# Hybrid decoder block: token sums on VectorE, g stored from GpSimd's queue, down products that share quarters taken in pairs

## The chip, the cores and the metric

One core of one Trainium2 chip runs the whole block. The metric is the device time of one execution in microseconds (us), the median of three runs. Engines: PE (TensorE matmul), DVE (VectorE), ACT (ScalarE), POOL (GpSimd), SP (SyncE, which here only issues DMAs); a q behind a name (SPq, POOLq) is that engine's DMA queue.

## The reference, cut to what matters

One block of depth 1 on 1024 tokens with 1024 features, all float32: a token mixer (pooling and sparse attention, not touched here), then the channel mixer and the last norm:

```python
def conv_ffn(xn, w_up, conv_w, conv_b, w_down):      # xn 1024x1024, D_FF = 2816
    h = xn @ w_up                                     # 1024 x 5632
    h = causal depthwise conv of width 3 over tokens (h) + conv_b
    a, b = jnp.split(h, 2, axis=-1)
    return (jax.nn.silu(a) * b) @ w_down              # 1024 x 1024

h = h + conv_ffn(rmsnorm(h, norm_ffn_g), w_up, conv_w, conv_b, w_down)
return rmsnorm(h, norm_final_g)
```

## The kernel before, in words

Everything is float32 by split operands: a value is kept as a rounded part hi (a cast on ACT, L50, L995, L1145) and the rest lo = value - hi (a subtraction on DVE or POOL, L51, L996, L1146), and a product is three matmuls, hi·hi, hi·lo, lo·hi (`mm3`, L82 to 87). The change touches the two functions of the channel mixer.

**ffn_up.** The 5632 columns of `w_up` are 44 blocks of 128, two to a chunk c (one of a, one of b). Chunk 0 (`plain`) is computed directly, as eight products. Chunks 1 to 21 (`pair`) take both blocks together with the two halves of the features and the two halves of the tokens as a 2x2 times 2x2 product in seven products in place of eight (Winograd's form). Each product is four `mm3`, so 12 matmuls of 128x128 by 128x512. For that, sums of quarters are wanted on both sides. On the weights' side each pair makes s1 to s4 (`combined`, L1070) and splits seven operands. On the tokens' side four sums T1 to T4 (for products 5, 6, 7 and 4, in the order of use) are made once, ahead of pair 1, in the loop that begins with `for k in range(4)`: T1 = x(0,1) - x(0,0), hi and lo parts alike, T2 = x(1,1) - T1, T3 = x(1,1) - x(0,1), T4 = x(1,0) - T2. T1, T2, T4 are DVE's (L1047 to L1052) and T3 POOL's; each quarter k of each sum is then split (L50, L51). The name tf stands for the float32 sums, T for the split ones. PE's products of a pair run in the order 1, 5, 2, 6, 7, 3, 4. Then `gated`: ACT applies the conv's tap of the token itself and the bias into acc (L1003), DVE adds two taps for each block (L1005, four instructions of 128x1023), ACT does silu (L1009), POOL multiplies into b (L1010), and SP stores b to the array gd in DRAM (L1011), 512 KB a chunk. The tile b has a single copy, so the next chunk's ACT step waits for that store.

**ffn_down.** g (from gd) times `w_down`, again as seven products of quarters, each over 11 blocks of the inner dimension in groups of two (five groups of two and one of one). Each group has one operand tile (`op`, three copies): quarters are loaded by SP (L1137, `raw`, twelve copies of 512 KB), POOL adds or subtracts where a product needs a sum (the `plan`, `plus`), ACT casts (L1145), DVE splits (L1146), and PE runs the group's matmuls on four banks (`steps`). In all 7 x 11 x 4 x 3 = 924 matmuls. Products 5, 6, 3 and 4 share running sums in `chs` and `cht`. The finished banks are added by DVE or POOL into h, which was loaded back from DRAM (L1202); `row_done` normalises a row with `rstd` (eleven small DVE instructions, L59 to L79) and two scalings on DVE (L1190) and stores it.

**Who sets the order.** PE's order is as written (`manual_schedule`). On all other engines a scheduler with its own cost model places the instructions, so the order of DVE, POOL, ACT and SP is not that of the code. Each engine and each queue then works strictly in that order.

## Time and profile before

| | |
|---|---|
| median of three runs | 1568.65 us (1568.16 to 1570.83) |
| the profiled execution | 1568.17 us, of which the trace's span is 1566.3 us |
| busy share of the span | PE 92%, DVE 77%, POOL 42%, ACT 41% |
| ffn_up's pairs and ffn_down | from about 849 us to the end |

The page of the profile gives busy time by engine, the span in 40 slices, the DMA queues, the chain of work that ended last, and the costliest groups of instructions. In a row of a timeline the first number is the start in us from the span's start, the second the busy us, then engine, line, operation, output<-inputs, form, count and, in brackets, the idle time before it and what ended that. Names of buffers stand without their numbers: `up` and `d` are PE's banks of the up and the down products, `w` a weight operand, `upr` a pair's loaded weights, `hr` the rows h at the end. An engine that waits shows idle time, not busy time. PE's share of 92% says little about any stage, so its waits have to be placed in time.

### The profile page before, as it was taken

The numbers are of one execution on the slowest core, as the hardware profiler recorded it, in microseconds if no ns is written. First come the engines' busy times: TensorE is split into PE (matmuls) and PEld (weight loads), VectorE is DVE, ScalarE is ACT, GpSimd is POOL, SyncE is SP. The second block draws the span as 40 slices with busy tenths as digits, with TensorE's granted clock in tenths as the row PEclk, the third lists the DMA queues.
The fourth block names the chain that finished last, engine by engine and source line by source line (L and its number), as shares of the span: only waits on it lengthen the run. The fifth ranks groups of instructions, "written<-read, shape, count | busy, mean of one in ns | idle before, by whom it ended". The sixth has DMA issues, their size and how long they took to land.

```text
span 1566.3 us, 18805 instructions
## 1 busy us (share of the span) xinstructions
PE 1433.6 (92%) x6658; PEld 1171.2 (75%) x6658; DVE 1209.4 (77%) x1875; ACT 647.0 (41%) x1111; POOL 664.4 (42%) x422
## 2 busy tenths in 40 slices
PE   6999999999899999998996499999999995898986
PEld 4887887887678788976875388888888884777765
DVE  7756999999941457876279988888888864799687
ACT  6655223213332567843033344444444433344242
POOL 4112424213522555443005754444444421778970
PEclk9999999999999999999998699999999997999998
DMA  8002423321115655166231122222222207966532
GB/s 333 8 29 91 141 76 109 123 72 41 54 74 195 186 164 162 28 214 207 86 129 40 41 81 81 81 81 81 81 81 81 81 27 292 414 220 227 202 108 108
DMA packets 77358, 193.12 MB, mean 123 GB/s; under 512 B 8784, under 2 KB 13776, under 8 KB 76752
## 3 DMA queue, kind: packets, MB, share of 16 engines
q1 hardware_dynamic: 71824, 179.34, 32.7%
q0 software_dynamic: 5440, 12.59, 2.8%
q8 instruction: 52, 0.85, 0.2%
q14 instruction: 42, 0.34, 0.1%
HBM read 148.90 MB, written 40.89 MB: 121 GB/s over the span
## 4 chain that ended last, share of the span: by engine, by line
PE 55%; DVE 30%; DMA 5%; issue 4%; POOL 3%; ACT 2%; SPq 0%; DVEq 0%; ACTq 0%; POOLq 0%
DVE tk_junk L554 11%; PE up L85 9%; PE up L87 9%; PE up L86 9%; DVE op L1146 6%; PE o L835 2%; PE pt L818 2%; PE d L86 2%; PE d L87 2%; PE d L85 2%; DVE tk_r L566 1%; DMA raw<-w_down 1%; DVE tk_cand L567 1%; PE is L439 1%; PE is L440 1%
## 5 line engine op out<-in xcount | busy, mean ns | idle before, releaser
L554 DVE TENSOR_SCALAR_CACHE_REDUCE tk_junk<-score,tk_cand 128x384 bf16<-128x384 f32 (+1 forms) x186 | 175.0, 941 | 1.8
L85 PE MATMUL up<-T,w 128*128 128x512 f32 x336 | 133.8, 398 | 30.5 <-ACT w L995 30.5
L1005 DVE SCALAR_TENSOR_TENSOR acc<-H,cw,acc 128x1023 f32<-128x1023 f32 x88 | 132.0, 1517 | 15.3 <-ACT acc L1003 14.5
L1146 DVE TENSOR_TENSOR op<-raw,op 128x1024 fp32r<-128x1024 f32 (+1 forms) x60 | 113.1, 1922 | 39.3 <-ACT op L1145 39.2
L86 PE MATMUL d<-op 128*128 128x512 f32 x308 | 125.2, 406 | 17.8 <-DVE op L1146 17.8
L85 PE MATMUL d<-op 128*128 128x512 f32 x308 | 123.7, 402 | 17.4 <-ACT op L1145 17.4
L87 PE MATMUL up<-T,w 128*128 128x512 f32 x336 | 133.6, 398 | 2.6 <-DVE w L996 2.6
L86 PE MATMUL up<-T,w 128*128 128x512 f32 x336 | 133.6, 398 | 0.0
L87 PE MATMUL d<-op 128*128 128x512 f32 x308 | 123.2, 400 | 0.0
L995 ACT CAST w<-s 128x512 fp32r<-128x512 f32 x84 | 52.0, 621 | 139.3 <-POOL s L1070 81.9
L996 DVE TENSOR_TENSOR w<-s,w 128x512 fp32r<-128x512 f32 x84 | 105.3, 1255 | 1.1
L85 PEld LDWEIGHTS up<-T,w 128*128 128x128 f32 x336 | 63.6, 189 | 46.1 <-ACT w L995 30.9
L1145 ACT CAST op<-raw 128x1024 fp32r<-128x1024 f32 (+1 forms) x60 | 56.2, 978 | 101.2 <-PE d L87 43.4
L1010 POOL TENSOR_TENSOR acc<-acc,acc 128x1024 f32<-128x1024 f32 x22 | 59.4, 2698 | 90.0 <-ACT w L995 69.6
L86 PEld LDWEIGHTS d<-op 128*128 128x128 f32 x308 | 60.0, 195 | 36.4 <-DVE op L1146 23.9
L996 POOL TENSOR_TENSOR w<-upr,w 128x512 fp32r<-128x512 f32 x23 | 36.7, 1600 | 112.4 <-DVE w L996 88.9
L85 PEld LDWEIGHTS d<-op 128*128 128x128 f32 x308 | 59.8, 194 | 31.2 <-ACT op L1145 18.3
L87 PEld LDWEIGHTS up<-T,w 128*128 128x128 f32 x336 | 63.5, 189 | 18.8 <-DVE w L996 3.4
L85 PE MATMUL up<-x2T,w 128*128 128x512 f32 x184 | 73.0, 397 | 2.3 <-ACT w L995 2.3
L86 PEld LDWEIGHTS up<-T,w 128*128 128x128 f32 x336 | 63.5, 189 | 15.2
L1070 POOL TENSOR_TENSOR s<-upr 128x512 f32<-128x512 f32 x42 | 55.9, 1331 | 42.3 <-DVE w L996 38.2
L825 DVE TENSOR_TENSOR PT<-pt,PT 128x512 fp32r<-128x512 f32 (+3 forms) x96 | 50.5, 554 | 29.8 <-ACT PT L824 29.4
(853 smaller groups left out, 4267.1 us busy)
## 6 DMA issues: line engine op xcount, KB each, us to landing
raw<-gd SPq DMA_DIRECT2D x45, 512.0 KB, 4.9
raw<-w_down SPq DMA_DIRECT2D x45, 512.0 KB, 5.5
upr<-w_up SPq DMA_DIRECT2D x44, 512.0 KB, 4.1
gd<-acc SPq DMA_DIRECT2D x22, 512.0 KB, 2.7
g<-gt SPq DMA_DIRECT2D x32, 256.0 KB, 2.0
xb<-x SPq DMA_DIRECT2D x8, 512.0 KB, 5.7
xTr<-xT SPq DMA_DIRECT2D x8, 512.0 KB, 6.4
mixd<-mixed SPq DMA_DIRECT2D x16, 256.0 KB, 2.6
```

The source lines that it names most:

```text
L85: t.matmul(ps, sh, mh, start=start, stop=False, skip_group_check=onto)
L86: t.matmul(ps, sh, ml, start=False, stop=False, skip_group_check=onto)
L87: t.matmul(ps, sl, mh, start=False, stop=stop, skip_group_check=onto)
L554: nc.vector.tensor_scalar(junk[:, :W], self.score[b], thr, None, op0=ALU.is_ge, op1=ALU.add, accum_out=cnt[:, j:j + 1])
L825: nc.vector.tensor_tensor(PT[:, j0:j1, 1, :], pt[:, 0:j1 - j0, :], PT[:, j0:j1, 0, :].bitcast(F32), op=ALU.subtract)
L995: nc.scalar.copy(t[:, 0], src)
L996: eng.tensor_tensor(t[:, 1], src, t[:, 0].bitcast(F32), op=ALU.subtract)
L1005: nc.vector.scalar_tensor_tensor(a[:, d:], H[o][:, 0:S - d], cw[:, n, 2 - d:3 - d], a[:, d:], op0=ALU.mult, op1=ALU.add)
L1010: nc.gpsimd.tensor_tensor(b, a, b, op=ALU.mult)
L1070: nc.gpsimd.tensor_tensor(t, a, b, op=op)
L1145: nc.scalar.copy(hi, val)
L1146: nc.vector.tensor_tensor(lo, val, hi.bitcast(F32), op=sub)
```

## The change

What it does, in four parts.

1. Token sums: all four on DVE, written one sum after another in the order of use (T1 and T2, then T3, then T4), with T2's float32 copy in a tile `t2f` that takes one of the two buffers of tag `raw` (the weights' of a pair). For pair 1 alone the weight sums and the last split, else POOL's, are DVE's too.
2. g is stored from POOL's queue in place of SP's.
3. ffn_down: products 1 and 5 run side by side, a group of each in turn, and 6 and 7 likewise. A quarter that both need is loaded once. All sums of quarters and all sums into h are DVE's. Four operand tiles in place of three, ten loaded quarters in place of twelve. h is loaded in four quarters of 1 MB, each written ahead of the product after which it is used.
4. The end: the last three groups in place of two are kept back and run bank by bank, the gain of the norm is multiplied ahead for two of the four quarters of h, of each row one half is scaled by ACT and one by DVE, and each half is stored by itself.

The diff, cut to its core:

```diff
@@ gated
-            nc.sync.dma_start(self.gd[c // NFH, :, :, c % NFH].rearrange("t p c -> p t c"),
-                              b.rearrange("p (t c) -> p t c", t=2))
+            nc.gpsimd.dma_start(self.gd[c // NFH, :, :, c % NFH].rearrange("t p c -> p t c"),
+                                b.rearrange("p (t c) -> p t c", t=2))
@@ ffn_up, token sums
-        for k in range(4):
-            xk = {q: [a[:, k] for a in v] for q, v in x.items()}
...
-            for n, a, b, eng in ((1, xk[0, 1], xk[0, 0], nc.vector), (3, xk[1, 1], xk[0, 1], nc.gpsimd)):
-                eng.tensor_tensor(f[n], a[0], b[0], op=sub)
-                eng.tensor_tensor(f[n], f[n], a[1], op=ALU.add)
-                eng.tensor_tensor(f[n], f[n], b[1], op=sub)
...
+        t2 = fw.tile([P, 4, HB], F32, tag="raw", name="t2f")
+        def difference(n, k, a, b):
+            f = pool.tile([P, HB], F32, tag=f"s{n}", name=f"tf{n}_{k}")
+            tt_(f, a[0], b[0], op=sub)
+            tt_(f, f, a[1], op=ALU.add)
+            tt_(f, f, b[1], op=sub)
+            return f
...
+        for k in range(4):
+            f = difference(1, k, xk((0, 1), k), xk((0, 0), k))
+            keep(1, k, f)
+            less(t2[:, k], xk((1, 1), k), f)
+            keep(2, k, t2[:, k])
+        for k in range(4):
+            keep(3, k, difference(3, k, xk((1, 1), k), xk((0, 1), k)))
+        for k in range(4):
+            f = pool.tile([P, HB], F32, tag="s4", name=f"tf4_{k}")
+            less(f, xk((1, 0), k), t2[:, k])
+            keep(4, k, f)
@@ pair
-                nc.gpsimd.tensor_tensor(t, a, b, op=op)
+                (nc.gpsimd if c > 1 else nc.vector).tensor_tensor(t, a, b, op=op)
...
-            operand_of(4, A[1, 1], nc.gpsimd)
+            operand_of(4, A[1, 1], nc.gpsimd if c > 1 else nc.vector)
@@ ffn_down
-        add, sub, plus = ALU.add, ALU.subtract, nc.gpsimd.tensor_tensor
+        add, sub, tt = ALU.add, ALU.subtract, nc.vector.tensor_tensor
...
+        def prepare_1_5(j, n):
+            A, B = quarters(j, n)
+            s, t = cs[:, j:j + n], ct[:, j:j + n]
+            p1, p5 = operand(1, j, n), operand(5, j, n)
+            put(p1, 0, A(0, 0))
+            b = B(0, 0)
+            put(p1, 1, b)
+            put(p5, 0, combined(s, A(1, 0), A(1, 1), add))
+            put(p5, 1, combined(t, B(0, 1), b, sub))
+            return p1, p5
...
+        def prepare_6_7(j, n):
...
+            a, b = A(0, 0), B(1, 1)
+            put(p6, 0, combined(s, s, a, sub))
+            put(p6, 1, combined(t, b, t, sub))
+            put(p7, 0, combined(a, a, A(1, 0), sub))
+            put(p7, 1, combined(b, b, B(0, 1), sub))
+            return p6, p7
...
-        def run(p, ps, first):
-            tail = 2 if p == 4 else 0
+        def run(prepare, pss, fresh, tail=0):
...
+                for t, ps in zip(ts, pss):
                     for tb in range(4):
-                        steps(ps, t, n, tb, first, k == 0, k == len(groups) - 1)
+                        steps(ps, t, n, tb, fresh, k == 0, k == len(groups) - 1)
...
+        def load_h(th, dh):
+            cols = slice(dh * HB, (dh + 1) * HB)
+            nc.sync.dma_start(h[:, 4 * th:4 * th + 4, cols], ...)
...
+            for dh in (1 - scaled, scaled):
+                q, cols = quarter(th, dh, tb), slice(dh * HB, (dh + 1) * HB)
+                if dh == scaled:
+                    nc.scalar.activation(q, q, AF.Copy, scale=y)
+                else:
+                    nc.vector.scalar_tensor_tensor(q, q, y, gfin[:, cols], op0=ALU.mult, op1=ALU.mult)
+                nc.sync.dma_start(io["out"][b * P:(b + 1) * P, cols], q)
...
-            run(1, x, True)
+            x, y = banks("x", 1), banks("y", 5)
+            run(prepare_1_5, (x, y), True)
...
-            run(4, x, False)
+            run(prepare_4, (x,), False, 3)
```

How it moves instructions, at three places.

DVE, where the token sums begin. `x2T1a` and `x2T1b` are the last token block of x, whose halves the sums wait for; before:

```order
L139 TENSOR_TENSOR x2T1a_7341<-hpt7_0_7598,x2T1a_7341 128x4x128
L1047 TENSOR_TENSOR tf1_0_7710<-x2T1a_7341,x2T00_6849 128x512
L139 TENSOR_TENSOR x2T1b_7342<-hpt7_4_7605,x2T1b_7342 128x4x128
L1048 TENSOR_TENSOR tf1_0_7710<-tf1_0_7710,x2T1a_7341 128x512
L1049 TENSOR_TENSOR tf1_0_7710<-tf1_0_7710,x2T10_6850 128x512
L1051 TENSOR_TENSOR tf2_0_7711<-x2T1b_7342,tf1_0_7710 128x512
L51 TENSOR_TENSOR T1_7706<-tf1_0_7710,T1_7706 128x512
```

and now:

```order
L139 TENSOR_TENSOR x2T1a_7341<-hpt7_0_7598,x2T1a_7341 128x4x128
L1048 TENSOR_TENSOR tf1_0_7711<-x2T1a_7341,x2T00_6849 128x512
L139 TENSOR_TENSOR x2T1b_7342<-hpt7_4_7605,x2T1b_7342 128x4x128
L1048 TENSOR_TENSOR tf3_0_7751<-x2T1b_7342,x2T1a_7341 128x512
L1049 TENSOR_TENSOR tf1_0_7711<-tf1_0_7711,x2T1a_7341 128x512
L1049 TENSOR_TENSOR tf3_0_7751<-tf3_0_7751,x2T1b_7342 128x512
L1050 TENSOR_TENSOR tf1_0_7711<-tf1_0_7711,x2T10_6850 128x512
L1050 TENSOR_TENSOR tf3_0_7751<-tf3_0_7751,x2T1a_7341 128x512
L1054 TENSOR_TENSOR t2f_7710<-x2T1b_7342,tf1_0_7711 128x512
L51 TENSOR_TENSOR T1_7706<-tf1_0_7711,T1_7706 128x512
L1055 TENSOR_TENSOR t2f_7710<-t2f_7710,x2T1b_7342 128x512
L51 TENSOR_TENSOR T3_7708<-tf3_0_7751,T3_7708 128x512
```

T3's sums, POOL's before, stand between T1's and T2's, in every quarter k. The end of the sums, now (before, `w1_5`, the operand of pair 1's product 5, stood two rows behind the last T2 split, and its sum s1 was POOL's):

```order
L51 TENSOR_TENSOR T1_7706<-tf1_3_7741,T1_7706 128x512
L51 TENSOR_TENSOR T3_7708<-tf3_3_7769,T3_7708 128x512
L1055 TENSOR_TENSOR t2f_7710<-t2f_7710,x2T1b_7342 128x512
L1086 TENSOR_TENSOR s1_1_7805<-upr1_7797 128x512
L1086 TENSOR_TENSOR s3_1_7818<-upr1_7797 128x512
L1054 TENSOR_TENSOR tf4_3_7790<-x2T00_6849,t2f_7710 128x512
L1086 TENSOR_TENSOR s2_1_7810<-s1_1_7805,upr1_7797 128x512
L51 TENSOR_TENSOR T2_7707<-t2f_7710,T2_7707 128x512
L996 TENSOR_TENSOR w1_5_7807<-s1_1_7805,w1_5_7807 128x512
```

The row of `w1_5` is the 64th, counted from the first sum, and T4's sums for k = 0 to 2 are done before it.

SP, where the down products begin. `gd` is g in DRAM, `raw` a loaded quarter (side and quarter in its name), `hr` h; before:

```order
L1011 DMA gd_7548<-acc43_10796 128x2x512
L1137 DMA raw1_000_10833<-gd_7548 128x1024
L1137 DMA raw1_010_10837<-w_down 128x1024
L1137 DMA raw1_200_10866<-gd_7548 128x1024
L1137 DMA raw1_210_10870<-w_down 128x1024
```

and now:

```order
L988 DMA upr21_10657<-w_up 128x1024 x2
L1226 DMA hr_10816<-hd_97 128x4x512
L1263 DMA gfin_10817<-norm_final_g 128x1024
L1226 DMA hr_10816<-hd_97 128x4x512 x3
L1138 DMA rawg00_0_10834<-gd_7548 128x1024
L1138 DMA raww00_0_10838<-w_down 128x1024
L1138 DMA rawg10_0_10842<-gd_7548 128x1024
L1138 DMA rawg11_0_10844<-gd_7548 128x1024
L1138 DMA raww01_0_10849<-w_down 128x1024
```

All of h and the gain stand ahead of the first quarter, directly behind the last weights, and the store of the last g is on POOL's queue. Quarter `g11` is the first that contains the last chunk of g.

DVE, at the end. `d7_3` is the last bank, f3 to f7 are rows 3 to 7 in `rstd`; before:

```order
L1234 TENSOR_TENSOR hr_10819<-d7_2_11687,hr_10819 128x512
L67 SCALAR_TENSOR_TENSOR f4t_12400<-f4y_12399,f4v_12398 128x1
L78 TENSOR_SCALAR f4t_12400<-f4t_12400 128x1
L59 TENSOR_SCALAR f5v_12418<-ssf5_11916 128x1
L79 TENSOR_TENSOR f4y_12399<-f4y_12399,f4t_12400 128x1
L1190 SCALAR_TENSOR_TENSOR hr_10819<-hr_10819,f4y_12399,gfin_10820 128x512 x2
L62 TENSOR_SCALAR f5t_12420<-f5v_12418 128x1
L1234 TENSOR_TENSOR hr_10819<-d7_3_11688,hr_10819 128x512
```

and now:

```order
L1298 TENSOR_TENSOR hr_10816<-d7_2_11451,hr_10816 128x512
L67 SCALAR_TENSOR_TENSOR f3t_12155<-f3y_12154,f3v_12153 128x1
L74 TENSOR_SCALAR f3u_12156<-f3t_12155 128x1
...
L79 TENSOR_TENSOR f3y_12154<-f3y_12154,f3t_12155 128x1
L1251 SCALAR_TENSOR_TENSOR hr_10816<-hr_10816,f3y_12154,gfin_10817 128x512
L62 TENSOR_SCALAR f4t_12368<-f4v_12366 128x1
L1298 TENSOR_TENSOR hr_10816<-d7_3_11452,hr_10816 128x512
L63 TENSOR_SCALAR f4y_12367<-f4t_12368 128x1
```

Before the last bank's sum stood row 4's scaling; now row 3's stands there and row 4's comes behind.

## Rows read from the trace of the kernel before

**Rows 1.** What PE waited for, 840 to 1567 us: total us, times, longest.
```profile
PE up L85 <- ACT w L995: 30.5, 1, 30.5
PE d L86 <- DVE op L1146: 17.8, 11, 3.4
PE d L85 <- ACT op L1145: 17.4, 2, 15.9
```

**Rows 2.** PE's timeline at the first up pair and the first down product.
```profile
879.37 0.79 PE L85 MATMUL up<-T,w 128*128 128x512 f32 x1 [30.46 <-ACT w L995]
...
883.24 0.80 PE L87 MATMUL up<-T,w 128*128 128x512 f32 x1 [2.65 <-DVE w L996]
...
1309.41 0.80 PE L85 MATMUL d<-op 128*128 128x512 f32 x1 [15.93 <-ACT op L1145]
```

**Rows 3.** DVE's timeline in the token sums.
```profile
831.36 0.68 DVE L1047 TENSOR_TENSOR tf<-x2T1a,x2T 128x512 f32<-128x512 f32 x1
...
837.67 1.77 DVE L1052 TENSOR_TENSOR tf<-tf,x2T1b 128x512 f32<-128x512 f32 x1
...
868.25 2.83 DVE L51 TENSOR_TENSOR T<-tf,T 128x512 fp32r<-128x512 f32 x1
```

**Rows 4.** Timelines of POOL and ACT, in the token sums and around the last chunk.
```profile
867.74 2.78 POOL L1010 TENSOR_TENSOR acc<-acc,acc 128x1024 f32<-128x1024 f32 x1
...
876.96 3.40 POOL L1070 TENSOR_TENSOR s<-upr 128x512 f32<-128x512 f32 x2
...
1298.83 2.34 POOL L1010 TENSOR_TENSOR acc<-acc,acc 128x1024 f32<-128x1024 f32 x1 [16.59 <-DVE acc L1005]
...
1294.73 1.24 ACT L1003 ACTIVATE acc<-H,cb,cw 128x1024 f32<-128x1024 f32 x1 [1.96 <-DVE H L1098]
...
1309.56 1.05 ACT L1145 CAST op<-raw 128x1024 fp32r<-128x1024 f32 x1 [0.20 <-DMA raw<-gd]
```

**Rows 5.** SP's timeline after the last chunk; the second number is the issue.
```profile
1301.20 0.36 SPq L1011 DMA_DIRECT2D gd<-acc  x1
...
1304.38 0.35 SPq L1137 DMA_DIRECT2D raw<-w_down  x1
```

**Rows 6.** DVE's timeline in the down products.
```profile
1309.39 6.23 DVE L1146 TENSOR_TENSOR op<-raw,op 128x1024 fp32r<-128x1024 f32 x5 [1.13 <-ACT op L1145]
...
1348.06 3.38 DVE L1146 TENSOR_TENSOR op<-cht,op 128x1024 fp32r<-128x1024 f32 x1
```

**Rows 7.** Windows: us, busy (x) of PE, PEld, DVE, ACT, POOL, PEclk, DMA, GB/s.
```profile
1309.00:1316.00 7.00, 6.13 (x14) 4.46 (x15) 6.12 (x5) 4.54 (x5) 0.00 (x0) 0.50 1.02 420
1340.00:1380.00 40.00, 35.61 (x155) 28.47 (x154) 31.02 (x14) 17.86 (x23) 31.34 (x12) 1.00 0.91 358
...
1309.40:1552.00 242.60, 222.96 (x924) 178.38 (x924) 198.47 (x163) 90.46 (x120) 167.41 (x64) 0.96 0.64 235
```

**Rows 8.** PE's timeline in the up products, 32 matmuls from the first to the last.
```profile
886.50 0.40 PE L86 MATMUL up<-T,w 128*128 128x512 f32 x1
...
893.97 0.40 PE L85 MATMUL up<-T,w 128*128 128x512 f32 x1
```

**Rows 9.** DMA issues: output<-input, queue, count, KB each, median us to landing.
```profile
upr<-w_up SPq DMA_DIRECT2D x44, 512.0 KB, 4.1
gd<-acc SPq DMA_DIRECT2D x22, 512.0 KB, 2.7
...
qA<-qd POOLq DMA_DIRECT2D x16, 256.0 KB, 3.7
...
mx<-mixd POOLq DMA_DIRECT2D x4, 1024.0 KB, 10.3
```

**Rows 10.** DVE's timeline at the end.
```profile
1552.33 0.68 DVE L1234 TENSOR_TENSOR hr<-d,hr 128x512 f32<-128x512 f32 x1
...
1554.57 1.41 DVE L1190 SCALAR_TENSOR_TENSOR hr<-hr,f5y,gfin 128x512 f32<-128x512 f32 x2
...
1557.73 1.41 DVE L1190 SCALAR_TENSOR_TENSOR hr<-hr,f6y,gfin 128x512 f32<-128x512 f32 x2
```

More of the change, by code (lines that the diff above doesn't have):

```diff
@@ L1203, in ffn_down @@
-            for tb in range(4):
-                nc.scalar.copy(r5[:, tb], y[tb])
-            run(2, x, False)
+                nc.scalar.copy(u2[:, tb], x[tb])
+            load_h(0, 0)
+            for tb in range(4):
+                nc.scalar.copy(u4[:, tb], y[tb])
+            run(prepare_2, (x,), False)
+            nc.sync.dma_start(gfin, io["norm_final_g"].partition_broadcast(P))
+            load_h(1, 1)
             for tb in range(4):
                 q = quarter(0, 0, tb)
-                nc.vector.tensor_tensor(q, x[tb], q, op=add)
+                tt(q, x[tb], q, op=add)
@@ L1209, in ffn_down @@
                 half_done(0, 0, tb)
-            y = banks("y", 6)
-            run(6, y, True)
+                gain(0, 0, tb)
+            y, x = banks("y", 6), banks("x", 7)
+            run(prepare_6_7, (y, x), True)
+            load_h(0, 1)
             for tb in range(4):
-                nc.vector.tensor_tensor(u2[:, tb], y[tb], r1[:, tb], op=add)
-                plus(r5[:, tb], r5[:, tb], u2[:, tb], op=add)
-                for th, dh, u in ((1, 1, r5), (0, 1, r5), (1, 0, u2)):
-                    q = quarter(th, dh, tb)
-                    plus(q, q, u[:, tb], op=add)
@@ L1224, in ffn_down @@
+                tt(q, q, u4[:, tb], op=add)
             y = banks("y", 3)
-            run(3, y, True)
+            run(prepare_3, (y,), True)
+            load_h(1, 0)
+            for tb in range(4):
+                q = quarter(1, 0, tb)
+                tt(q, q, u2[:, tb], op=add)
             for tb in range(4):
                 q = quarter(0, 1, tb)
-                nc.vector.tensor_tensor(q, y[tb], q, op=add)
+                tt(q, y[tb], q, op=add)
                 half_done(0, 1, tb)
-                row_done(0, tb)
```

119 lines of the change are left out of this document (62 added, 57 removed).

## Prediction

> **What bounds the kernel now.** I read the waits of the matrix engine (PE) first, over the last 727 us. Nearly all its idle time there is in three places [rows 1, 2]: one wait of 30.5 us and one of 2.6 us where the second half of the network (the up products) begins, 17.4 us on ACT's casts of which 15.9 stand in one piece where the down products begin, and eleven short ones, 17.8 us in all, on DVE's splits inside the down products.
>
> The first place: PE resumes at 883.24 [rows 2]. The operand it waits for is made from a weight sum that POOL begins at 876.96, because POOL first finishes its share of the token sums [rows 4]. DVE meanwhile is busy without a pause, but at two speeds: a 128x512 sum takes 0.68 us while POOL is idle and 1.77 us beside a POOL sum; beside POOL's 2.78 us product one split took 2.83 us [rows 3, 4].
>
> The second place: the last up product ends at about 1293.5, its g leaves POOL at 1301.2 (1298.83 + 2.34), and only then does SP, which stores g, come to the loads behind the store; the second load waits for the store to land and goes at 1304.38, and PE starts at 1309.41 [rows 2, 4, 5].
>
> The third place: a 128x1024 split takes 1.22 us when POOL is idle (6.12 us for five, with the DMA engines moving 420 GB/s) and 3.38 us beside a POOL sum [rows 6, 7]. So both engines crawl in step, and PE waits for each second operand. After the 15.9 us gap PE's granted clock is 0.50, so 1.2 in place of 2.4 GHz: 14 matmuls in 6.13 us, 0.44 each [rows 7], where 32 in the up products take 7.47 us, 0.233 each [rows 8]. In all the 924 matmuls of the down products stand in 242.6 us [rows 7]; at 0.233 they would take 215.6, so 27.0 us are lost there.
>
> **Token sums (first place).** POOL's 16 instructions go to DVE; it issues 56 in place of 40, and pair 1's four weight sums and one split as well. The order shown above is not the order of use: T3's sums stand beside T1's and T4's between them, and the first operand of product 5 is the 64th row counted from the first sum. Those are 60 of 128x512 and four convolution steps of 128x1023. At the undisturbed rate (0.61 and 1.22 us, a fifth of the five splits) that is 36.6 + 4.9 = 41.5 us. The first sum stands at 831.36 [rows 3]; it moves about 1 us ahead, since pair 1's first split and four matmuls no longer stand before it. One POOL piece is left in this stretch, the product of plain chunk 0, which costs DVE 2.83 - 0.61 = 2.2 us. So 830.4 + 41.5 + 2.2 = 874.1, against 883.24: 9.1 us saved. ACT must keep up: chunk 0's accumulator needs PE's last blocks. PE's long wait begins at 879.37 - 30.46 = 848.9 [rows 2], after pair 1's first 12 matmuls (2.8 us), so those blocks are there near 846, while DVE comes to that row after 20 sums, near 842.6; at worst DVE waits 5 us there (gain 4). With no POOL product at all the gain would be 11. The float32 copy of T2 also takes one of the two weight buffers, so pair 2's weights are loaded only after T4, and land 4.1 us later [rows 9], near 880; PE comes to pair 2 about 17 us after 874, and the sixth product of pair 1 waits at most a microsecond longer behind DVE's first pair-2 splits. **Term: -9, between -11 and -4.**
>
> **g stored from POOL's queue.** In the up products PE is never short of anything, so 21 of the 22 stores only change places. The buffer of b has one copy: ACT fills it at 1294.73, the store goes at 1301.20 and lands 2.7 us later, 9.2 us in all [rows 4, 5, 9], of a pair's 84 matmuls of 0.233 us = 19.6 us [rows 8]. There are 10 us of slack, and an issue on POOL adds about half a microsecond.
>
> **Start of the down products (second place).** By the order, SP now issues four 1 MB loads of h and the gain first, as soon as T2's and T3's buffers are free, at two and three products of 2.8 us before the up products end (near 1285 and 1288 on the old clock), then three quarters that wait for the last up product alone, and then one that waits for the last store. 4.7 MB at 358 GB/s [rows 7] is 13 us, so h is in near 1299, the first two quarters 2.9 us later, and with some 1 us to land and a cast of 1.05 [rows 4] PE begins near 1304: 5 us ahead of 1309.41. Its first 24 matmuls last 14 x 0.44 + 10 x 0.233 = 8.5 us, to 1312.5. Product 5's first operand hangs on the last store. No row has a store of 512 KB from POOL; the nearest are 2.7 us for the same tile from SP and 3.7 us for a 256 KB load from POOL [rows 9]; I take 3.7. Then 1301.2 + 0.5 + 3.7 + 4.1 (load) + 2.4 (two sums) + 1.05 (cast) + 1 (the split before) = 1314, so 1.5 us of wait. **Term: -4;** h at 420 GB/s and a quick store give -8, h at 300 GB/s and a store like the 10.3 us of the 1 MB loads from POOL give +3. The Trainium skill, page "DMA: Bandwidth & Descriptors", section "Anatomy of one DMA — SWDGE (gpsimd) path", fits such a transfer as 2.0 us plus bytes over 436 GB/s, an estimate of 3.2 us here; by it the term would be -4.5. No run so far shows it.
>
> **Down products (third place).** Products 1 and 5 now share the load of B(0,0), 6 and 7 those of A(0,0) and B(1,1): 15 loads of a group in place of 18. All 48 combinations go from POOL to DVE, and POOL has no row left after the last store. DVE's load: 84 splits and 48 sums, 110 of 128x1024 and 22 of half that, 121 x 1.22 = 148 us; 44 sums of 128x512 for h, u2 and u4, 27 us; four of the eight row scales, about 10 us. That is 185 us beside PE's 215.6 us. By stage: products 1 and 5, 6 rows of 1.22 in 11.2 us of PE; 2, 2.4 in 5.6; 6 and 7, 8 rows, 9.8 in 11.2; 3 and 4, 3.7 in 5.6 and the h sums besides. The tightest is products 6 and 7, where some of their sums already stand within product 2 in DVE's order, and four operand buffers hold two pairs. ACT casts 14 rows a group, 14.7 us in 39. So I take the waits of this stage as gone, and the slow clock behind them: of the 27.0 us lost only the slow start stays, 14 x (0.44 - 0.233) = 2.9 us, which leaves 24. I keep 2 us for waits that I don't see. **Term: -22,** between -24 (none) and -12 (half stay).
>
> **The end.** The last group is kept back over three groups in place of two, and half of each row is scaled by ACT. Before, the last sum from PSUM starts at 1552.33 and the rows follow at 3.16 us each [rows 10], to the span's end at 1566.3, 14 us. In the order, rows 4 to 7 still stand behind the last sum from PSUM, row 4 whole where before it was half done; each is shorter by one 0.7 us scale. One row more and 4 x 0.7 less: **0, within 1.5.**
>
> **Sum.** -9 - 4 - 22 + 0 = -35. The profiled execution took 1568.17 us with a span of 1566.3, so 1531.3 + 1.9 = 1533 us. The median of the three runs is 0.5 us above that execution, which changes nothing here.
>
> **Rivals.**
> *DVE is late in spite of its average* (chance 0.09). It works in order, and its order puts sums far ahead of splits that PE needs now; in product 3 some 20 h sums stand between two splits. For it: the average load is 86%. Against it: by stage it stays under PE's time. If half of the third place's gain is lost: 1545 us.
>
> *The transfers bind* (0.06). Products 1 and 5 ask for 5 x 0.52 MB in 11.2 us, 234 GB/s, after 4.7 MB of h. If the chip gave 250 GB/s, h would land 5.7 us later, the first ten quarters 6 us later, and what is lost would not be made up before product 2: some 18 us, 1551. Against it: 358 and 420 GB/s in the rows [rows 7].
>
> *Stores from POOL starve* (0.04), the one that ends slower. The place is the single buffer of b. If a store lands more than 2.7 + 10 = 12.7 us after its product, ACT waits, then DVE, then PE, in each of 21 pairs. The nearest row with a bad value is 10.3 us, for 1 MB loads four at a time [rows 9]. Each microsecond beyond 12.7 costs 21; from 14.4 on the whole gain of 35 is gone, and at 16 the time is 1533 + 69 = 1602. The Trainium skill, page "SBUF — State Buffer", section "Who interferes with whom", says that a DMA which seems stalled by a DVE operation was issued by GpSimd and starved of descriptor time. The same section adds, as inferred, that a tensor_tensor does not do this, and DVE has mostly those here. The rows agree so far in that loads from POOL beside a busy DVE land in 3.7 us.
>
> *Nothing moves* (0.01): each gain is eaten by a wait right behind it, 1568.
>
> **How the numbers follow.** My forecast has 0.80. Its own terms reach from -47 to -15, and all at one end is unlikely, so I take 1524 to 1542 for it. With the late DVE the range is 1524 to 1549, which leaves out the other rivals and a little of the forecast. A measurement here tells 0.2%, about 3 us: faster 0.80 + 0.09 + 0.06 = 0.95, same 0.01, slower 0.04.
>
> **What would show it.** PE's wait before product 5 of pair 1 about 24 us, and DVE's 128x512 sums near 0.68 us throughout. A first down matmul about 11 us after the last up matmul, then one wait of 1 to 3 us. DVE's splits of 128x1024 near 1.2 us with no POOL rows beside them, and no wait of PE above 1 us until the end. The end about as long as before. I am wrong if PE waits for DVE in products 6, 7 or 3, if the h loads hold the first operand beyond 14 us, or if accumulators wait for stores.

## The result, and the profile after

The changed kernel takes 1533.32 us (median of 4 runs, 1530.82 to 1533.77), the kernel before beside it 1568.41 us (4 runs, 1567.64 to 1570.83): 0.977 of it, with an interval of 0.9753 to 0.9787. 1533 was forecast. The profiled execution took 1532.94 us with a span of 1530.8, against 1566.3 before: 35.5 us less. The whole came out as forecast. Of its terms one, the down products, came out beyond its range, and the token sums gave back part of what they had won.

What PE waited for in the same stretch as in [rows 1], 830 us to the end, after the change (total us, times, longest):

```profile
PE up L85 <- ACT w L995: 20.3, 1, 20.3
PE d L85 <- ACT op L50: 11.6, 2, 10.7
...
PE d L86 <- DVE op L51: 1.3, 2, 0.8
...
```

The wait of 30.5 us is 20.3, the 15.9 before the down products 10.7, and the eleven waits on splits, 17.8 us, are two of 0.8 and 0.5. One wait has grown: before product 3 of pair 1, the sixth of that pair's seven, PE lost 1.2 us, now 2.5.

That wait before, and PE's timeline after, where [rows 2] answer to it, with that wait and the first down products:

```profile
896.77 0.47 PE L85 MATMUL up<-x2T1b,w 128*128 128x512 f32 x1 [1.24 <-DVE u L1092]
```

```profile
872.99 0.79 PE L85 MATMUL up<-T,w 128*128 128x512 f32 x1 [20.34 <-ACT w L995]
875.35 0.79 PE L87 MATMUL up<-T,w 128*128 128x512 f32 x1 [1.14 <-DVE w L996]
891.47 0.77 PE L85 MATMUL up<-x2T1b,w 128*128 128x512 f32 x1 [2.53 <-DVE u L1108]
...
1300.40 0.80 PE L85 MATMUL d<-op 128*128 128x512 f32 x1 [10.69 <-ACT op L50]
...
1309.25 0.50 PE L85 MATMUL d<-op 128*128 128x512 f32 x1 [0.86 <-ACT op L50]
1310.57 0.50 PE L86 MATMUL d<-op 128*128 128x512 f32 x1 [0.81 <-DVE op L51]
```

DVE's timeline after in the token sums (answers to [rows 3]):

```profile
860.15 0.69 DVE L1054 TENSOR_TENSOR t2f<-x2T1b,tf 128x512 f32<-128x512 f32 x1
...
878.34 2.75 DVE L1086 TENSOR_TENSOR s<-upr,s 128x512 f32<-128x512 f32 x1
881.83 4.18 DVE L996 TENSOR_TENSOR w<-s,w 128x512 fp32r<-128x512 f32 x1 [0.74 <-ACT w L995]
```

POOL's there (answers to [rows 4]):

```profile
858.00 22.53 POOL L1010 TENSOR_TENSOR acc<-acc,acc 128x1024 f32<-128x1024 f32 x1 [30.32 <-DVE acc L1005]
...
881.65 2.56 POOL L1086 TENSOR_TENSOR s<-upr 128x512 f32<-128x512 f32 x2
```

DVE keeps one speed, 0.60 us from start to start, from 834 to 878. But POOL's one product there, 2.78 us before, takes 22.5 us, and pair 2's weight sums stand behind it. It ends beside DVE's next row, at 878.34, which takes 2.75 us in place of 0.69, and beside POOL's first weight sums for pair 2 DVE's split at 881.83 takes 4.18.

SP's timeline from the last up products (answers to [rows 5]), and the DMA issues of g (answers to [rows 9]; KB each, median us to landing):

```profile
1284.56 1.54 SPq L1226 DMA_DIRECT2D hr<-hd  x3
...
1291.37 10.82 SPq L1138 DMA_DIRECT2D rawg<-gd  x2
```

```profile
gd<-acc POOLq DMA_DIRECT2D x22, 512.0 KB, 3.2
```

DVE in the down products (answers to [rows 6]), and windows with the columns of [rows 7]: the first 40 us of the down products and all of them.

```profile
1341.77 1.22 DVE L51 TENSOR_TENSOR op<-cht,op 128x1024 fp32r<-128x1024 f32 x1
```

```profile
1300.00:1340.00 40.00, 37.47 (x148) 29.79 (x149) 32.87 (x30) 16.90 (x18) 0.00 (x0) 0.90 0.96 370
1300.40:1516.50 216.10, 213.73 (x924) 175.47 (x924) 174.03 (x221) 92.72 (x124) 0.00 (x0) 0.98 0.59 202
```

No row of 3.38 us is left: all splits and sums of 128x1024 take 1.22. What a matmul of the down products takes where PE does not wait is read from the starts. PE's timelines, 32 matmuls from the first row of each view to the second, before and then after:

```profile
1320.65 0.39 PE L85 MATMUL d<-op 128*128 128x512 f32 x1
...
1327.91 0.39 PE L87 MATMUL d<-op 128*128 128x512 f32 x1
```

```profile
1450.14 0.39 PE L85 MATMUL d<-op 128*128 128x512 f32 x1
...
1457.40 0.39 PE L87 MATMUL d<-op 128*128 128x512 f32 x1
```

In both kernels that is 7.26 us, 0.227 each; in the up products it is 7.47 us, 0.233 each [rows 8], and so it is after.

The end after, DVE's last sum from PSUM (answers to [rows 10]):

```profile
1516.31 0.69 DVE L1298 TENSOR_TENSOR hr<-d,hr 128x512 f32<-128x512 f32 x1 [0.51 <-PE d L87]
```

**By stage.** A span is cut at four places: t0, the start of DVE's last split of a token block (line 139, 830.75 us before); the end of the last up matmul; the end of the last down matmul; the end of the span. What lies before t0 is the same code in all kernels here, and yet t0 falls between 829.7 and 839.6, so small totals are read by stage. Each ratio is to the runs of the kernel before that were made beside that kernel.

| kernel | t0 | t0 to the last up matmul | to the last down matmul | to the end | median us (runs) | ratio, interval |
|---|---|---|---|---|---|---|
| before | 830.75 | 462.74 | 258.21 | 14.60 | 1568.41 (4) | |
| after | 833.60 | 456.11 | 226.56 | 14.53 | 1533.32 (4) | 0.977, 0.9753 to 0.9787 |
| tsums | 830.03 | 461.09 | 254.12 | 14.86 | 1566.74 (12) | 0.9984, 0.9966 to 1.0002 |
| sp_store | 829.73 | 459.73 | 228.26 | 14.68 | 1536.49 (3) | 0.9792, 0.9769 to 0.9815 |
| c0_dve | 839.62 | 453.19 | 224.48 | 14.61 | 1529.79 (4) | 0.9746, 0.9721 to 0.9771 |
| t_order | 830.49 | 468.70 | 224.68 | 14.53 | 1541.64 (6) | 0.9825, 0.9796 to 0.9854 |
| t_order_c0 | 834.52 | 467.18 | 224.45 | 14.55 | 1542.13 (4) | 0.9829, 0.9807 to 0.985 |
| down_pool | 831.57 | 456.12 | 253.96 | 13.05 | 1561.22 (4) | 0.9946, 0.9925 to 0.9967 |
| woven | 831.48 | 455.89 | 224.48 | 14.55 | 1530.26 (4) | 0.9761, 0.9728 to 0.9793 |
| gd_split_h_late | 830.93 | 456.12 | 226.21 | 14.64 | 1531.08 (4) | 0.9763, 0.9738 to 0.9788 |
| b_low | 837.65 | 454.60 | 221.39 | 14.56 | 1525.9 (4) | 0.9717, 0.9684 to 0.9749 |
| tail_rows | 834.34 | 456.17 | 230.88 | 9.41 | 1531.73 (4) | 0.9755, 0.9736 to 0.9773 |
| all_three | 832.52 | 451.81 | 221.78 | 9.39 | 1517.29 (5) | 0.9666, 0.9651 to 0.968 |

Where the code of a stage is the same, the up stage agrees within 0.06 us (after, down_pool, gd_split_h_late, tail_rows), the down stage within 2.1 (after, c0_dve, t_order, t_order_c0, woven). One kernel stands apart: b_low's edit adds no instruction to the up stage, and that stage is 1.5 us shorter. PE's timeline of b_low at product 3 of pair 1:

```profile
895.53 0.47 PE L85 MATMUL up<-x2T1b,w 128*128 128x512 f32 x1 [3.27 <-DVE u L1111]
```

Product 3 starts 57.9 us after t0 there, as in the changed kernel. But the row lasts 0.47 us in place of 0.77: the granted clock stayed at 1.00 over the wait, where in the changed kernel it stood at 0.50 for some 3 us behind it. So 1.5 us of an up stage can come or go with the clock alone.

### The profile page after: what moved, and what is told of

It reads as the page before. It is cut to its first block, busy times and chain, and to the rows that moved or that the text cites. A ratio compares the mean times of both kernels' runs of the same rounds, so it can differ in the third digit from the quotient of the medians.

```text
span 1530.8 us, 18757 instructions
## 1 busy us (share of the span) xinstructions
PE 1431.6 (94%) x6658; PEld 1173.2 (77%) x6658; DVE 1177.1 (77%) x1960; ACT 652.7 (43%) x1119; POOL 491.8 (32%) x359
## 4 chain that ended last, share of the span: by engine, by line
PE 64%; DVE 26%; DMA 3%; issue 3%; ACT 3%; POOL 1%; SPq 0%; DVEq 0%; ACTq 0%; POOLq 0%
DVE tk_junk L554 11%; PE up L85 9%; PE up L86 9%; PE up L87 9%; PE d L86 4%; PE d L87 4%; PE d L85 4%; PE o L835 2%; PE pt L818 2%; DVE tk_r L566 2%; DVE tk_cand L567 1%; PE is L439 1%; PE is L440 1%; PE wvp L86 1%; PE wvp L85 1%
## 5 line engine op out<-in xcount | busy, mean ns | idle before, releaser
L85 PE MATMUL up<-T,w 128*128 128x512 f32 x336 | 134.0, 399 | 20.3 <-ACT w L995 20.3
L85 PE MATMUL d<-op 128*128 128x512 f32 x308 | 121.4, 394 | 11.6 <-ACT op L50 11.6
L86 PE MATMUL d<-op 128*128 128x512 f32 x308 | 121.3, 394 | 1.3 <-DVE op L51 1.3
L87 PE MATMUL d<-op 128*128 128x512 f32 x308 | 120.8, 392 | 0.0
L1010 POOL TENSOR_TENSOR acc<-acc,acc 128x1024 f32<-128x1024 f32 x22 | 79.1, 3593 | 120.5 <-ACT w L995 70.8
L85 PE MATMUL up<-x2T,w 128*128 128x512 f32 x184 | 74.4, 405 | 2.3 <-ACT w L995 2.3
L86 PEld LDWEIGHTS up<-T,w 128*128 128x128 f32 x336 | 63.7, 190 | 15.2
L87 PE MATMUL up<-x2T,w 128*128 128x512 f32 x184 | 74.1, 403 | 0.0
L86 PE MATMUL up<-x2T,w 128*128 128x512 f32 x184 | 74.1, 402 | 0.0
L1003 ACT ACTIVATE acc<-H,cb,cw 128x1024 f32<-128x1024 f32 x44 | 54.8, 1246 | 35.6 <-DVE H L1114 24.4
```

What stands on the lines that cost most here:

```text
L85: t.matmul(ps, sh, mh, start=start, stop=False, skip_group_check=onto)
L86: t.matmul(ps, sh, ml, start=False, stop=False, skip_group_check=onto)
L87: t.matmul(ps, sl, mh, start=False, stop=stop, skip_group_check=onto)
L1003: nc.scalar.activation(a, H[o], AF.Identity, bias=cb[:, n:n + 1], scale=cw[:, n, 2:3])
L1010: nc.gpsimd.tensor_tensor(b, a, b, op=ALU.mult)
```

## The experiments

**tsums: the token sums alone.** The kernel before with the first part of the change; the stores stay on SP, the down products as they were.

```diff
+        t2 = fw.tile([P, 4, HB], F32, tag="raw", name="t2f")
...
+        for k in range(4):
+            f = difference(1, k, xk((0, 1), k), xk((0, 0), k))
+            keep(1, k, f)
+            less(t2[:, k], xk((1, 1), k), f)
+            keep(2, k, t2[:, k])
...
-                nc.gpsimd.tensor_tensor(t, a, b, op=op)
+                (nc.gpsimd if c > 1 else nc.vector).tensor_tensor(t, a, b, op=op)
```

> The kernel before with the first part of the change alone: token sums all on DVE, t2f in a weight buffer, pair 1's weight sums and last split on DVE. Theory A (the prediction): the part is worth 9 us, 1568.4 - 9 = 1559.4. Theory B, from the trace of the changed kernel: from the first token sum to the last up product it has 455.5 us where before had 462.1, so 6.6 us, 1561.8, because POOL's product of chunk 0 lasts 22.5 us beside a DVE that never pauses, POOL's weight sums of pair 2 come late, and product 3 of pair 1 waits 2.5 us. Below 1560.5 speaks for A, above for B. By both DVE's 128x512 sums take about 0.69 us throughout; B also expects POOL's product of chunk 0 to last over 15 us here.

Both theories miss. The first operand comes 9.2 us earlier, as in the whole change (t0 + 39.37 against + 48.62), and POOL's product is as long as theory B has it, but the stage is only 1.65 us shorter, and the median does not tell it from before. SP's and POOL's timelines of tsums show what takes it back:

```profile
876.97 0.38 SPq L1011 DMA_DIRECT2D gd<-acc  x1
877.40 25.75 SPq L988 DMA_DIRECT2D upr<-w_up  x6
```

```profile
854.42 22.52 POOL L1010 TENSOR_TENSOR acc<-acc,acc 128x1024 f32<-128x1024 f32 x1 [29.57 <-DVE acc L1005]
884.61 2.49 POOL L1086 TENSOR_TENSOR s<-upr 128x512 f32<-128x512 f32 x2 [7.67 <-DMA upr<-w_up]
```

Chunk 0's product takes 22.52 us on POOL, SP waits with its store at the head of the queue, and pair 2's weight loads stand behind that store. POOL then waits 7.67 us for them and PE 6.60 before product 3 of pair 1.

**sp_store: the whole change with the store back on SP.**

```diff
-            nc.gpsimd.dma_start(self.gd[c // NFH, :, :, c % NFH].rearrange("t p c -> p t c"),
+            nc.sync.dma_start(self.gd[c // NFH, :, :, c % NFH].rearrange("t p c -> p t c"),
```

> The changed kernel with one edit undone: g is stored from SP's queue again. In SP's order the store of chunk 0 then stands ahead of the loads of pair 2's weights, and the last store ahead of the first quarter of the down products. Theory A (the prediction): 21 of the 22 stores only change places, so from the last token block's first split on DVE to the end of the last up product the stage stays at 456 us, as in the changed kernel; only the start of the down products changes. Theory E: pair 2's weights are loaded only when POOL has finished the product of chunk 0, which DVE starves; the stage becomes as long as in the run with the token sums alone, 461 us, and POOL waits some 8 us for weights. By both the gap between up and down products grows from 10.7 to about 15 us, and product 5 follows with a shorter wait. Total by A 1534 to 1537, by E 1539 to 1542.

SP's timeline in sp_store shows the same queue as in tsums:

```profile
876.68 0.38 SPq L1011 DMA_DIRECT2D gd<-acc  x1
877.12 2.95 SPq L988 DMA_DIRECT2D upr<-w_up  x4
```

In the changed kernel those loads go 41.1 us after t0 (874.72), here 47.4 us after it, and POOL waits 7.6 us for them. The up stage, 459.73 us, is 3.6 us longer, nearer to theory E; the total lies in A's range. The gap between up and down products is 15.3 us, as both had it, and the down stage is 1.7 to 3.8 us longer than the five readings of the same code. So POOL's queue for the store is worth some 5 to 7 us in these traces; the medians differ by 3.2, with intervals that overlap.

**c0_dve: chunk 0's product on DVE.**

```diff
-            nc.gpsimd.tensor_tensor(b, a, b, op=ALU.mult)
+            (nc.vector if c == 0 else nc.gpsimd).tensor_tensor(b, a, b, op=ALU.mult)
```

> The changed kernel with one instruction moved: the product of chunk 0 (silu(a) * b) by DVE in place of POOL. Theory A: DVE's list before product 5 gets 1.2 us longer, no wait goes away: 1533.3 to 1534.5. Theory B: POOL is free when pair 2's weights land, its weight sums and DVE's splits come earlier, the 2.5 us wait at product 3 of pair 1 goes with about 1.6 us of slow clock behind it, less 1.2 us: about 3 us faster, 1530.4.

The first operand comes 1.1 us later (t0 + 40.51), by the product that now stands in DVE's row. But the wait before product 3 falls from 2.53 to 0.56 us, and the stage from 456.11 to 453.19, 9.55 us below before. PE's and DVE's timelines of c0_dve there:

```profile
896.07 0.47 PE L85 MATMUL up<-x2T1b,w 128*128 128x512 f32 x1 [0.56 <-DVE u L1108]
```

```profile
885.48 0.69 DVE L1086 TENSOR_TENSOR s<-upr,s 128x512 f32<-128x512 f32 x1
886.91 1.51 DVE L996 TENSOR_TENSOR w<-s,w 128x512 fp32r<-128x512 f32 x1 [0.74 <-ACT w L995]
```

The two rows of DVE that took 2.75 and 4.18 us take 0.69 and 1.51, and product 3 starts 56.5 us after t0 in place of 57.9. This shows that the starved product made PE wait longer there, worth 1.4 us. The other 1.5 us are the clock behind that wait (the row lasts 0.47 us in place of 0.77): b_low got them with the product starved and a longer wait, so c0_dve does not show that they belong to the product.

**t_order: DVE's token sums strictly in the order of the code; t_order_c0: the same with chunk 0's product on DVE.**

```diff
+        def tt_(*args, **kw):
+            then(nc.vector.tensor_tensor(*args, **kw))
...
-            self.split(f, T[n][:, 0, k], T[n][:, 1, k])
+            nc.scalar.copy(T[n][:, 0, k], f)
+            tt_(T[n][:, 1, k], f, T[n][:, 0, k].bitcast(F32), op=sub)
```

> The changed kernel with the token sums chained in the order that the code writes, T1 and T2, then T3, then T4; nothing else is tied, other DVE work may stand between. The operand of product 5 becomes the 39th row counted from the first sum, in place of the 64th. Theory C: PE's wait for product 5 sets this stage; that product starts about 12 us earlier, PE then waits for T3 and T4 in smaller pieces, the last of T4 ends where it ended, product 3 starts some 8 us earlier: 1525. Theory D: the length of the whole list sets it, the last T4 split and the weights of pair 2 that wait for the buffer of t2f end where they did, so pair 2 starts no earlier: 1531 to 1533.

> Both of the two edits before: token sums chained in written order, and the product of chunk 0 by DVE. Theories B and C together: 8 + 3 us, 1522. If B is wrong and C right, 1525 to 1526. If C is wrong (theory D) and B right, 1530. POOL's weight sums of pair 2 should begin when its weights land, and product 3 of pair 1 should not wait for a DVE sum for more than 1 us.

Both miss: the first operand comes earlier by 5.9 and 6.9 us (t0 + 33.49, + 32.48), and the stage is 12.6 and 11.1 us longer. DVE's, PE's and POOL's timelines of t_order:

```profile
858.55 0.69 DVE L1054 TENSOR_TENSOR tf<-tf,x2T1a 128x512 f32<-128x512 f32 x1
859.27 0.69 DVE L1054 TENSOR_TENSOR tf<-tf,x2T 128x512 f32<-128x512 f32 x1
860.65 0.69 DVE L1054 TENSOR_TENSOR T<-tf,T 128x512 fp32r<-128x512 f32 x1 [0.69 <-ACT T L1069]
...
894.26 0.69 DVE L1098 TENSOR_TENSOR s<-upr,s 128x512 f32<-128x512 f32 x1
```

```profile
895.71 0.79 PE L85 MATMUL up<-x2T1b,w 128*128 128x512 f32 x1 [7.01 <-ACT w L995]
```

```profile
854.74 2.63 POOL L1010 TENSOR_TENSOR acc<-acc,acc 128x1024 f32<-128x1024 f32 x1 [29.41 <-DVE acc L1005]
```

A sum that needs the one before it starts 0.72 us after it, not 0.60, and each split waits some 0.7 us for ACT's cast of the sum just made. The list gets longer: the last split of T4 ends 63.7 us after t0, in the changed kernel 44.7. Two of pair 1's own weight sums stand behind T3's and T4's sums (882.24 and 894.26), and PE waits 7.26 and 7.01 us for the operands made from them; t_order_c0 has the same two waits. T2's copy also holds its weight buffer longer, and pair 2's weights come late: POOL gets them at 896.92, in the changed kernel it began at 881.65. In the changed kernel the mixed order covers both pauses: its rows start every 0.60 us. In the pauses POOL's product takes 2.63 us: it is not the product that is slow.

**down_pool: the 48 quarter sums of the down products back on POOL.** Pairing, shared loads and row scales stay as changed.

```diff
-            tt(dst, a, b, op=op)
+            nc.gpsimd.tensor_tensor(dst, a, b, op=op)
```

> The changed kernel with the 48 sums of quarters of the down products back on POOL, the shared loads, the pairing and the sums into h as changed. Theory A (the prediction): a split beside a POOL sum takes 3.4 us in place of 1.2, 48 of them, so PE waits again in most groups of products 5, 6, 7, 3 and 4; from the first to the last down matmul 230 to 243 us (before 242, changed 216). Theory F: sharing and pairing are what removed the waits, and POOL's sums run in the pauses of DVE: 216 to 222 us.

The down stage is 253.96 us, against 258.21 before and 226.56 changed. DVE's and POOL's timelines of down_pool:

```profile
1341.85 2.32 DVE L51 TENSOR_TENSOR op<-cht,op 128x1024 fp32r<-128x1024 f32 x1
1344.09 1.21 DVE L51 TENSOR_TENSOR op<-rawg,op 128x1024 fp32r<-128x1024 f32 x1
```

```profile
1340.81 2.28 POOL L1149 TENSOR_TENSOR cht<-raww,raww 128x512 f32<-128x512 f32 x1
```

Beside POOL's sum a split takes 2.32 us (others up to 3.4), as soon as POOL is idle 1.21. The down matmuls take 243.7 us from first to last, just above theory A's range and far from F's. The 4.3 us that are left against before are the earlier start (a gap of 10.28 for 15.92 us); the matmuls themselves take 1.4 us more than before. So the gain of the down products themselves is that POOL has no row there; products that share loads bring nothing without it. What they bring together with it was not tried apart.

**gd_split_h_late: g in one scratch tensor for each two chunks, and the loads of SP in the order of the code, h behind the first quarters.**

```diff
-        self.gd = dram("gd", [2, 2, P, NFH, HB])
+        self.gd = {(f, j): dram(f"gd{f}{j}", [2, P, min(2, NFH - j), HB]) for f in range(2) for j in range(0, NFH, 2)}
...
+        def fetch(dst, src):
+            ins = nc.sync.dma_start(dst, src)
+            if loads:
+                self.tc.add_manual_dep(ins.ins, loads[-1].ins.name,
...
```

> The changed kernel with two edits at the start of the down products: g in DRAM as one array for each half and group in place of a single one, so that a quarter waits only for the stores that it holds; and SP's loads of ffn_down tied in the order of the code, so that the 4 MB of h and the gain come after the quarters of products 1 and 5. Theory H: h ahead of the quarters holds PE's start by about 4 us, and the last store holds product 5: the gap between up and down falls from 10.7 to about 7 us, product 5 starts without a wait, the first 24 matmuls are followed at once; span about 5 to 6 us less in these two stages (gap + down 226.6 us in the changed kernel, now 221). Theory I: the transfers bind here anyway (404 GB/s in the gap): the h loads only move into products 1 and 5 and make PE wait there, gap + down 225 to 227.

The gap before the first down matmul falls from 10.69 to 6.8 us, but the matmuls then take 219.40 us from first to last, in place of 215.87: 226.21 in all, no gain, as theory I has it. SP's timeline of this kernel:

```profile
1288.70 10.80 SPq L1137 DMA_DIRECT2D rawg<-gd  x2
```

SP still stands 10.8 us at the third quarter of g, though nothing that the last store writes is read by it any more. So it did not wait for the data. By the layout its buffer overlaps the last chunk's b, which the last store still reads, so it may wait for space; the next run tries that.

**b_low: the same, with b's buffer placed where no early quarter overlaps it.**

```diff
+        for o in (1, 0):
+            pool.tile([P, S], F32, tag=f"acc{o}", name=f"place{o}")
```

> As gd_split_h_late, with the tile of b placed first in its pool, by allocating its tag ahead of the others; no instruction is added. Theory J: in the changed kernel and in gd_split_h_late the load of quarter g11 of the first group waits for the last store not for its data but for its space: its buffer overlaps the tile of b, which the store reads (addresses 113408 to 117504 against 110048 to 114144), and all later loads stand behind it on SP. With b lower, the first six quarters wait for nothing later than DVE's last read of the H tiles, some 5 us after the last up product; product 5 then follows the first group of product 1 without a wait above 0.5 us, gap + down 226.2 us in gd_split_h_late becomes about 222. Theory I: the transfers bind in products 1 and 5, PE waits for quarters somewhere there, gap + down stays 225 to 227.

SP's timeline of b_low:

```profile
1293.90 3.85 SPq L1139 DMA_DIRECT2D rawg<-gd  x2
```

PE now has two waits, 7.5 us before the first operand and 1.3 at the second, the one before product 5 is gone, and the stage takes 221.39 us, 4.8 less than gd_split_h_late, as theory J has it. It was space. (That its up stage is shorter too is not the edit's doing, see By stage.)

**tail_rows: rows 0 to 3 of the last norm taken as one batch, ahead of DVE's wait for the last product.**

```diff
+                if tb == 0:
+                    ss["y"] = self.rstd(pool, ss["all"], "f03", n=4, halves=True)
+                y = ss["y"][:, tb:tb + 1]
```

> The changed kernel with the last norm's rows 0 to 3 taken together: their eleven small instructions once for four rows in place of four times, all ahead of the first sum of product 4 on DVE. Theory K: in the changed kernel DVE stood 2.8 us at the first of product 4's sums with rows 1 to 3 queued behind it, so rows 4 to 7 came after the last sum, 14.5 us from the last matmul to the end. Now each of rows 4 to 6 is done while PE works on the next bank, one row is left behind the last sum: 8 to 9 us from the last matmul to the end, the whole 6 us less than the changed kernel. Theory L: the end is set by the stores and the wait for them, 12 us or more.

The end is 9.41 us, 5.1 less, near the 8 to 9 of theory K. But the down stage grew to 230.88 us, 4 to 6 more than its like. SP's timeline of tail_rows, and its window to set beside the changed kernel's first 40 us:

```profile
1306.55 0.48 SPq L1141 DMA_DIRECT2D rawg<-gd  x1
...
1308.86 6.56 SPq L1229 DMA_DIRECT2D hr<-hd  x3
```

```profile
1300.00:1340.00 40.00, 34.85 (x124) 27.17 (x125) 22.04 (x20) 12.17 (x12) 0.02 (x1) 0.85 0.97 378
```

With this edit the order of SP's loads, which the build sets, came out otherwise: h stands among the quarters that products 1 and 5 wait for. From 1300 to 1340 PE made 124 matmuls, in the changed kernel 148. That the new place of h is the cause was not tried by itself.

**woven: two blocks of sums side by side in a fixed order, chunk 0's product on DVE.** Each block's rows stand between the other's, so that no sum follows the one it needs.

```diff
+        def spare(n, k):
+            tag = {1: ("s3", "s4"), 2: ("u2", "u4"), 3: ("s3", "s4"), 4: ("r1", "s4")}[n][k % 2]
+            return pool.tile([P, HB], F32, tag=tag, name=f"tf{n}_{k}")
...
+        for thread in (first, third, fourth):
+            weave(thread, (0, 1))
+            weave(thread, (2, 3))
```

> As c0_dve, with the token sums tied in an order of use that weaves two quarters k: T1 and T2 of k 0 and 1, then of k 2 and 3, then T3, then T4, in two threads, so that a split never stands right behind its own sum; pair 2's splits stand behind pair 1's sums from PSUM. The tiles of the float32 sums take other tags so that two of a kind can be live. Theory G (why the written order was slower): there each split waited about 0.7 us for ACT's cast of the sum just before it, and each sum for the one before; woven, the list is as short as in the changed kernel (T4's last split about 45 us after the first), product 5 starts about 26 us after the first split of the last token block in place of 40, and the stage to the end of the last up product is 448 to 450 us (c0_dve 453.2, changed 456.1). Theory D: the length of DVE's whole list sets the end, pair 1's last products still wait for it: 452 to 454 us, with more and shorter waits of PE.

The stage takes 455.89 us, no better than the changed kernel and outside both theories. PE's longest wait says why:

```profile
PE up L85 <- ACT r L1148: 19.5, 1, 19.5
```

That was a slip in the edit: half of T4's sums lie in the buffer r1, which ACT needs for the copies out of PSUM, so PE's next chunk waited for the last token sums. The run says nothing on the order itself.

**all_three: woven without that slip, with the edits of b_low and of tail_rows.** T4's sums lie in a buffer of chunk 0's accumulator.

```diff
+        four = pool.tile([P, S], F32, tag="acc0", name="tf4")
+        weave(fourth, (0, 1))
+        weave(fourth, (2, 3))
```

> The changed kernel with all repairs: the product of chunk 0 by DVE, the token sums woven by two quarters in the order of use (T4's float32 sums in a tile of the accumulators, so that no tile that pair 1 needs early is held), pair 2's splits behind T4; the start of the down products as in b_low; the end as in tail_rows. From the first split of the last token block to the end of the last up product: theory G (the list is as short as the changed one's, products 5, 2, 6, 7, 3 run while it ends) 448 to 450 us, theory D (DVE's whole list sets the end) 452 to 454, changed 456.1. With J and K, total about 17 us below the changed kernel, 1516; with D, I and L about 3 below, 1530.

What PE waited for in all_three, 830 to 1300 us:

```profile
PE up L88 <- ACT w L1000: 6.9, 1, 6.9
...
PE up L89 <- DVE T L1054: 4.1, 1, 4.1
PE up L88 <- ACT r L1157: 3.7, 1, 3.7
...
PE up L88 <- DVE u L1163: 1.2, 1, 1.2
PE up L90 <- DVE w L1001: 0.5, 1, 0.5
```

Three waits of 23.9 us in the up products have become five of 16.4 us, 4.3 us of the stage against the changed kernel and only 1.4 against c0_dve, no more than the clock alone made in b_low. The stage, 451.81 us, lies below D's 452 to 454 and above G's 448 to 450. DVE's list is not shorter for the weaving: the last split of T4 ends 50.9 us after t0, in c0_dve 45.8. So that the order itself brings anything is not shown. With 221.78 and 9.39 us in the other stages this is the version that beats both, 1517.29 us, 0.9666 of before (0.9651 to 0.968); with G, J and K 1516 was expected.

## Why the prediction held, point by point

From -9 - 4 - 22 + 0 = -35 came -6.6 - 5.2 - 26.4 - 0.1 and 2.9 of a later t0, -35.5 in all. The sum is right, and it owes that in part to errors of opposite sign.

**Token sums, forecast -9, measured -6.6.** The first step held. The row with the forecast 874.1 came at 875.35 with t0 2.85 us later, so 10.7 us earlier than before on one clock, where 9.1 were forecast. Then 4.1 us were given back. The step that failed is the one that let POOL's product of chunk 0 cost DVE 2.2 us ahead of product 5. There it cost DVE nothing and POOL 20 us. DVE paid at the product's end, 2.1 us at the row at 878.34, and POOL came late to the sums of pair 2, beside which DVE's split took 4.18 us. Likewise the sixth product of pair 1, "at most a microsecond longer" behind DVE, waited 1.3 us longer, and the granted clock fell behind that wait, which it did not before (a first row of 0.77 us against 0.47). Windows of PE, before and after, the first 20 us from the second operand on (columns as in [rows 7]):

```profile
883.24:893.24 10.00, 10.00 (x37) 8.06 (x38) 9.86 (x8) 4.29 (x9) 8.66 (x6) 0.86 0.01 2
893.24:903.24 10.00, 8.77 (x38) 6.84 (x37) 8.10 (x9) 3.30 (x5) 5.84 (x5) 1.00 0.29 105
```

```profile
875.35:885.35 10.00, 10.00 (x32) 7.93 (x33) 9.22 (x7) 3.90 (x7) 9.69 (x5) 0.71 0.45 159
885.35:895.35 10.00, 7.47 (x26) 5.67 (x25) 8.06 (x10) 1.24 (x2) 5.29 (x5) 0.83 0.28 105
```

A window counts the matmuls that reach over its ends as well. By their starts, PE began 74 matmuls in these 20 us before and 56 now: 18 x 0.233 = 4.2 us, as much as was given back. By parts, from the starts after t0: until PE was ready for product 3 it lost 1.3 us, at the lower clock at first (0.71 in place of 0.86; in the kernel before more of the slow time lay inside the wait, 2.65 us [rows 2] in place of 1.14); 1.3 us in the longer wait; 1.5 us at the lower clock behind it (0.83 in place of 1.00). A wait that was shortened here gave less than its length. The last part is chance as much as it is the change: b_low, with the same code there, did not have it. c0_dve, without the starved product, gives 9.55 us for this term.

**g from POOL's queue, forecast: 21 of 22 stores only change places.** This step failed, to the good. The first of those stores mattered: on SP it stands ahead of pair 2's weight loads and waits for the starved product (tsums, sp_store). I had counted what each store is late for, and not what stands behind it. Without it the first part of the change would be worth 1.65 us. That stores do not starve held: 3.2 us each. The Trainium skill, page "DMA: Bandwidth & Descriptors", section "Anatomy of one DMA — SWDGE (gpsimd) path", gives an estimate of 3.2 us for this size, and the trace agrees; I had taken 3.7.

**Start of the down products, forecast -4, measured -5.2.** PE began 10.7 us after the last up matmul, as the text said it should (about 11), and the two waits of product 5 were 0.86 + 0.81 us (1.5 forecast). The h loads held the first operand as forecast: without them in front the gap is 6.8 us. But the wait at product 5 had a reason beside the one given, which held it just as long: not only was its data tied to the last store, its buffer lay over the last b, which that store reads (gd_split_h_late against b_low).

**Down products, forecast -22 between -24 and -12, measured -26.4.** The mechanism held: splits at 1.22 us, no waits of PE over 0.9 us, DVE 174 us where 185 were reckoned, and down_pool shows that POOL's absence does it. The size was off, beyond the end of the range, because the floor was: I took the 0.233 us a matmul of 32 up products [rows 8] for the least. That is right for the up products, but the down products take 0.227 where nothing holds them, and the trace of the kernel before has this too. So 924 of them need 209.5, not 215.6, and 242.3 - 209.5 = 32.8 us were lost before, not 27. Of these 6.4 are still lost after, where 4.9 were reckoned: 13 matmuls at the lower clock stand 0.43 us apart (2.6 us), the wait at the very first second operand and the two of product 5 come to 2.1 (0.46, 0.86, 0.81), and the rest are slow matmuls next to these waits.

**The end, forecast 0, measured -0.1.** From DVE's last sum to the end of the span it takes 14.5 us (1516.31 to 1530.8), before 14.0 (1552.33 [rows 10] to 1566.3): the whole row behind the last sum and the shorter scales cancel within 0.6 us, as reckoned.

**The rivals.** DVE was not late in the down products. Over all of them the transfers took 0.59 of the DMA engines, 202 GB/s. In the first 40 us they came near to binding, 0.96 and 370 GB/s, and PE waited for product 5 alone; with h among the quarters (tail_rows) it waited more often. Stores landed after 3.2 us, too soon to hold the single buffer of b.

## What to carry to other kernels

When work is taken off one of two engines that slow each other, look for the single piece that is left on it: it may get no turn at all, and what matters then is what stands behind it, on its own engine and on every queue that waits for it in order. A wait before a load can be for space as well as for data, and the two look alike in a trace until one is taken away. A floor of time per instruction is taken from a steady stretch of the same stage, and not from the stage next to it.

## What the runs showed of the hardware that was not expected

**A piece on POOL can starve behind DVE.** In the kernel before the two engines took turns: sums of 1.6 to 1.8 us on POOL, 1.77 on DVE. When DVE's rows followed each other every 0.60 us without a pause, 33 of them, POOL's product of two SBUF operands lasted 22.5 us in each of the seven kernels that kept it on POOL with the sums in that order (22.50 to 22.54). Where DVE paused 0.69 us, in t_order, it lasted 2.63. The Trainium skill, page "SBUF — State Buffer", section "Who interferes with whom", says that a DVE instruction with two SBUF inputs contends with a GpSimd instruction that reads SBUF, and that the order of issue decides which of the two blocks. The contention agrees with the trace (22.5 us for 2.63). But POOL did not get in between two DVE instructions here: it lost to the whole row of them.

**Matmuls of one shape at one granted clock differ.** At a granted clock of 1.00 the starts of 128x512 matmuls stand 0.233 us apart in the up products and 0.227 in the down products of the same execution, before and after. Why stays open.
